# A fused transformer kernel: the first block's 3-tap convolution in PSUM, and the state space tiles turned through DRAM

## The chip, the cores and the metric

The kernel runs on one core of one Trainium2 chip, as one program. The metric is the device time of one execution in microseconds; differences below are against the kernel before, which already holds its 31-tap convolution (second block) in PSUM.

The engines, as the profile names them: PE (TensorE, matmuls; PEld its weight loads), DVE (VectorE), ACT (ScalarE), POOL (GpSimd), SP (SyncE, here the queue that issues most DMAs). ACT and POOL have DMA queues too.

## The reference

512 tokens, 1024 channels, all float32. The first block has two layers. Layer 0 mixes with a gated MLP and attention; layer 1 with a state space model (S5): 64 groups of 16 channels, each with 64 complex states.

```python
def s5_mixer(u, a_re, a_im, log_dt, b_re, b_im, c_re, c_im, d):
    ...                                   # ab = exp(lambda*dt), bb = discretized B
    bu_re = jnp.einsum('gpc,bsgc->bsgp', bb_re, uf)
    bu_im = jnp.einsum('gpc,bsgc->bsgp', bb_im, uf)
    _, _, xr, xi = lax.associative_scan(_complex_affine_combine, (a_r, a_i, bu_re, bu_im), axis=1)
    y = einsum('gcp,bsgp->bsgc', c_re, xr) - einsum('gcp,bsgp->bsgc', c_im, xi) + d * uf
# layer 1:
g_a, g_b = jnp.split(jax.nn.gelu(y) @ od_w_glu[o], 2, axis=-1)
x = x + g_a * jax.nn.sigmoid(g_b)
# both layers then run
def conv_ffn(x, w_up, conv_w, conv_b, w_down):
    h = x @ w_up                          # 1024 -> 2 * 2816
    hc = conv_b + conv_w[0] * hp[:, 0:seq] + ...   # 3 taps over time, per channel
    g, up = jnp.split(hc, 2, axis=-1)
    return (jax.nn.silu(g) * up) @ w_down
x = x + sigmoid(rms_norm(x) @ ple_w_gate[i]) * (p[i] @ ple_w_proj[i])
```

The second block (SwiGLU FFN, a mixer with retention and a 31-tap convolution, SwiGLU FFN, layer norms) is not touched.

## The kernel before, in words

Activations lie channel-major: a tile `x[k]` is 128 channels x 512 tokens, eight of them. Every large matmul is made of three: activations and weights are split into a rounded high part and a low rest (`split`, L290: ACT rounds, DVE or POOL subtracts; weights in `cook`, L328 and L331), and PE adds high x high, high x low, low x high (`mm_fm`, L354 to L356). PSUM has eight banks of 128 x 512 floats; a tile of `bank()` takes one and gives it back after its last use. Weights come on SP's queue through two raw buffers, one piece ahead (`fetch`, L310).

A scheduler orders the instructions of each engine when the program is built: it takes the order of the code as priority, but pulls ahead what it reckons to be ready earlier. On the chip every engine and every DMA queue runs its list in order.

`conv_ffn` (L812) runs three parts of 8, 8 and 6 channel tiles. In a part, each step `c` makes a pair of tiles: 48 matmuls for the gate half (s=0), 48 for the up half (s=1), each into two banks. DVE multiplies a bank by the norm's row `rb` into an SBUF tile `hs` (L839), ACT makes the newest tap with the bias (L841), DVE adds two taps that read `hs` shifted (L845); ACT makes Silu of the gate half (L849), POOL (DVE in the last step of a part) multiplies the two (L851), and `split` hands the product to the down projection. In layer 0 a callback `side()` inserts the preparation of the state space tables between these steps: mostly POOL products (L1147 to L1151), and on PE the transposes and small matmuls of `finish` (L1108, L1115). The 16 finished tables, 128 x 1920 floats each, are kept in DRAM (`tabs`).

The state space layer runs eight units, one per channel tile, software-pipelined over `t`: `load` (six DMAs on SP bring the unit's tables `tG`, `tE`, `tC`, two buffers each), `drive`, `mid`, `scan`, `emit`, and the first GLU column block for the unit's tile. A unit works on blocks of four tokens: 32 channels x 4 tokens on the partitions, 4 channel groups x 128 blocks along the row. `drive` therefore turns the normed tile `h` (L1215) into `up` by 16 copies of 32x128 (L1222, L1224); `mid` multiplies by `tG` on PE (L1231) and rotates on DVE (L1234 to L1237) and POOL (L1239, L1240); `scan` runs two scans on DVE (L1250) and rotates back on DVE and POOL (L1256 to L1261); `emit` sums three matmuls (L1269) and turns the result back inside 16 Gelus of 32x128 (L1274), then splits it into `G`. The first GLU column block (both halves, s=1 and s=0, 12 matmuls per unit) accumulates unit by unit in four banks; blocks 1 to 3 follow densely, then sigmoid, product and addition to `x` (L1319 to L1321), then `conv_ffn` of layer 1.

Of the kernel before, what the change touches and what calls it, by code (L numbers as in the profile page):

```python
# [18 lines left out]
P = 128  # L19
T = 512  # L20
# [29 lines left out]
def tile_net(ctx: ExitStack, tc: tile.TileContext, a, out):  # L50
# [764 lines left out]
    def conv_ffn(l, X, rms, side):  # L815
        Xn = None
        with tc.tile_pool(name=nm("ffn"), bufs=1) as fp:
            rb = None
            for t0, nt in PARTS:
                A = act_tiles(fp, "A", nt)  # L820
                for c in range(nt // 2):
# [12 lines left out]
                    for j in range(2):  # L834
                        cv = []
                        for s in range(2):
                            ch = s * KF + m0 + j
                            hs = fp.tile([P, T], F32, tag=f"hs{s}", name=nm("hs"), bufs=2)
                            vec.tensor_tensor(hs, accs[s][j], rb, op=ALU.mult)  # L839
# [10 lines left out]
                        eng = vec if c == nt // 2 - 1 else pool  # L850
                        eng.tensor_tensor(cv[0], cv[0], cv[1], op=ALU.mult)  # L851
                        split(A.h[2 * c + j], A.l[2 * c + j], cv[0])
# [95 lines left out]
    tabs = [dr.tile([P, 2 * TAB], F32, tag=f"tab{i}", name=f"tab{i}") for i in range(16)]  # L948

# [241 lines left out]
    with tc.tile_pool(name="s5r", bufs=1) as rp:  # L1191
        G = act_tiles(rp, "G", KD)
# [4 lines left out]
        class Unit:  # L1197
# [14 lines left out]
            def drive(self):  # L1212
                k = self.k
                h = rp.tile([P, T], F32, tag="h", name=nm("h"))
                vec.scalar_tensor_tensor(h, x[k], col("norm_mix", KD + k), rb2, op0=ALU.mult, op1=ALU.mult)  # L1215
                hv = h.rearrange("p (n j) -> p j n", j=4)
                self.up = up = rp.tile([P, 4, P], F32, tag="up", name=nm("up"), bufs=3)
                for b in range(4):
                    for i in range(4):
                        d, s = up[32 * b:32 * b + 32, i, :], hv[32 * i:32 * i + 32, 3 - b, :]  # L1220
                        if k < 3 and i % 2:
                            vec.tensor_copy(d, s)  # L1222
                        else:
                            act.copy(d, s)  # L1224

            def mid(self):
                k, up = self.k, self.up
                pv = [bank((P, 4, P)) for _ in range(2)]
                for z in range(2):
                    for i in range(4):  # L1230
                        pe.matmul(pv[z][:, i, :], self.G[:, i, P * z:P * z + P], up[:, i, :], start=True, stop=True)  # L1231
                er, ei = self.E[:, :, 0:P], self.E[:, :, P:]
                t = self.t = [xt_(f"X{'hl'[self.par]}{j}") for j in range(4)]
                vec.tensor_tensor(t[0], er, pv[0], op=ALU.mult)  # L1234
                vec.tensor_tensor(t[1], ei, pv[1], op=ALU.mult)
                vec.tensor_tensor(t[2], er, pv[1], op=ALU.mult)
                vec.tensor_tensor(t[3], ei, pv[0], op=ALU.mult)  # L1237
                eng = pool if k else vec
                eng.tensor_tensor(t[0], t[0], t[1], op=ALU.add)  # L1239
                eng.tensor_tensor(t[2], t[2], t[3], op=ALU.subtract)  # L1240
                self.rm = xt_(f"X{'hl'[self.par]}5")
                vec.tensor_copy(self.rm, r4[:, 4 * k:4 * k + 4].unsqueeze(2).to_broadcast([P, 4, P]))
                pool.memset(self.rm[:, :, 0:1], 0.0)

            def scan(self):
                k, t = self.k, self.t
                er, ei = self.E[:, :, 0:P], self.E[:, :, P:]
                zr, zi = xt_("Xh4"), xt_("Xl4")
                for z, w in ((zr, t[0]), (zi, t[2])):
                    vec.tensor_tensor_scan(z.rearrange("p i n -> p (i n)"), self.rm.rearrange("p i n -> p (i n)"),  # L1250
                                           w.rearrange("p i n -> p (i n)"), 0.0, op0=ALU.mult, op1=ALU.add)
# [4 lines left out]
                vec.tensor_tensor(t[1], er, zr, op=ALU.mult)  # L1256
                vec.tensor_tensor(t[3], ei, zi, op=ALU.mult)
                (pool if k % 3 else vec).tensor_tensor(self.xr[:, :, 1:], t[1], t[3], op=ALU.subtract)
                pool.tensor_tensor(t[0], er, zi, op=ALU.mult)
                pool.tensor_tensor(t[2], ei, zr, op=ALU.mult)  # L1260
                pool.tensor_tensor(self.xi[:, :, 1:], t[0], t[2], op=ALU.add)  # L1261

            def emit(self):
# [6 lines left out]
                y = rp.tile([P, T], F32, tag="y", name=nm("y"), bufs=2)  # L1270
                yv = y.rearrange("p (n j) -> p j n", j=4)
                for i in range(4):
                    for r in range(4):
                        act.activation(yv[32 * i:32 * i + 32, r, :], py[32 * r:32 * r + 32, i, :],  # L1274
                                       AF.Gelu_apprx_tanh)
                split(G.h[k], G.l[k], y)

        units = [Unit(k) for k in range(KD)]
        units[0].load()
        units[0].drive()  # L1280
        acc0, w0s = {}, {}
        for t in range(KD + 3):
            if t + 1 < KD:
# [3 lines left out]
            if t + 1 < KD:  # L1287
                units[t + 1].drive()
            if 0 <= t - 1 < KD:
                units[t - 1].scan()  # L1290
            if t == 2:
                for s in (1, 0):
                    w0s[s] = W(hold=s == 0)
                    acc0[s] = [bank() for _ in range(2)]
            if 0 <= t - 2 < KD:
                units[t - 2].emit()
            if 0 <= t - 3 < KD:
                k = t - 3
                for s in (1, 0):
                    mm_fm(acc0[s], w0s[s], G, [k], start=k == 0, stop=k == KD - 1, js=[k])  # L1300
            if t == KD:
# [4 lines left out]
                fetch(nxt[0] + 1)  # L1306

        X = new_x()
        rms = Rms()
        for c in range(4):  # L1310
# [5 lines left out]
            for j in range(2):  # L1316
# [4 lines left out]
                vec.tensor_tensor(x[m], x[m], sg, op=ALU.add)  # L1321
# [490 lines left out]
```

## Time and profile before

| | us |
|---|---|
| median of 3 runs (lowest, highest) | 2843.62 (2843.29, 2844.3) |
| profiled execution, device time | 2841.44 |
| its span (first to last instruction) | 2839.7 |
| PE busy | 2725.4 (96%) |
| DVE busy | 1628.6 (57%) |
| ACT busy | 1075.9 (38%) |
| POOL busy | 729.5 (26%) |
| mean granted TensorE clock | 0.98 |

The profile is of one execution. Busy is the share of time in which an engine has an instruction in work; PE's matmuls overlap, so PE can be busy without being at its peak. [...] In rows, `a<-b,c` is the written tile and the tiles read, a number after `x` is a count, and square brackets hold the idle time before an instruction and what ended it. Times of day are us from the span's start. The chain of waits follows the work that ended last backwards, at each step to whatever released it.

### The profile page before, as it was taken

How to read it: one execution, taken by the hardware profiler on the slowest of the kernel's cores; microseconds unless marked ns; L12 is line 12 of the kernel's file. 1: busy time of each engine (PE TensorE's matmuls, PEld its weight loads, DVE VectorE, ACT ScalarE, POOL GpSimd, SP SyncE). 2: the span in 40 equal slices, each digit the busy share in tenths (PEclk: the TensorE clock that was granted, in tenths of full speed). 3: DMA queues.
4: the chain of work that ended last, by engine and by line, in shares of the span. 5: the costliest groups of instructions: out<-in, count | busy, mean ns of one | idle time of the engine just before them, and what ended most of it. 6: DMA issues, size and time to landing. Idle time of an engine off the chain costs nothing.

```text
span 2839.7 us, 35255 instructions
## 1 busy us (share of the span) xinstructions
PE 2725.4 (96%) x14363; PEld 2297.3 (81%) x14363; DVE 1628.6 (57%) x2527; ACT 1075.9 (38%) x1503; POOL 729.5 (26%) x621
## 2 busy tenths in 40 slices
PE   9999999999679999999999998999999899999998
PEld 8978887877567888888888887887888778889898
DVE  6456968685774655466333336866387664733335
ACT  5544424344594433244312124333333253431222
POOL 2214046772351001012000025343443321300000
PEclk9999999999689999999999999999999999999999
DMA  5203323433532223224232222222222223232222
GB/s 159 75 30 105 111 95 138 151 124 133 191 97 97 96 89 104 89 89 134 89 104 90 97 82 73 86 95 80 95 80 95 75 89 104 76 104 89 90 90 75
DMA packets 266323, 281.44 MB, mean 99 GB/s; under 512 B 18917, under 2 KB 257479, under 8 KB 266160
## 3 DMA queue, kind: packets, MB, share of 16 engines
q1 hardware_dynamic: 246992, 256.18, 27.4%
q10 hardware_dynamic: 18336, 22.58, 2.2%
q8 instruction: 113, 1.85, 0.3%
q0 software_dynamic: 832, 0.41, 0.1%
q14 instruction: 50, 0.41, 0.0%
HBM read 259.23 MB, written 19.92 MB: 98 GB/s over the span
## 4 chain that ended last, share of the span: by engine, by line
PE 82%; DVE 6%; POOL 5%; ACT 4%; issue 2%; DMA 1%; SPq 0%; POOLq 0%; ACTq 0%; DVEq 0%
PE ps L355 22%; PE ps L354 22%; PE ps L356 22%; PE ps L363 4%; PE ps L365 4%; PE ps L364 4%; ACT y L1274 2%; DVE ps L1478 1%; ACT up L1224 1%; POOL abd L1151 1%; POOL tb L1147 1%; POOL tb L1148 1%; POOL tabs L1151 1%; PE ps L635 1%; PE ps L1539 1%
## 5 line engine op out<-in xcount | busy, mean ns | idle before, releaser
L328 ACT CAST whi<-raw 128x2048 fp32r<-128x2048 f32 (+2 forms) x216 | 406.1, 1880 | 733.5 <-PE ps L355 569.1
L354 PE MATMUL ps<-Xh,whi 128*128 128x512 f32 (+1 forms) x1472 | 570.9, 389 | 3.3 <-ACT whi L328 1.8
L355 PE MATMUL ps<-Xl,whi 128*128 128x512 f32 (+1 forms) x1472 | 566.6, 385 | 3.5 <-POOL Xl L294 3.4
L356 PE MATMUL ps<-Xh,wlo 128*128 128x512 f32 (+1 forms) x1472 | 565.9, 385 | 2.4 <-DVE wlo L331 2.4
L331 DVE TENSOR_TENSOR wlo<-raw,whi 128x2048 fp32r<-128x2048 f32 (+2 forms) x167 | 381.4, 2284 | 321.5 <-ACT whi L328 317.7
L331 POOL TENSOR_TENSOR wlo<-raw,whi 128x2048 fp32r<-128x2048 f32 (+1 forms) x49 | 223.3, 4556 | 688.5 <-ACT whi L328 376.7
L354 PEld LDWEIGHTS ps<-Xh,whi 128*128 128x128 f32 x1472 | 278.5, 190 | 62.2 <-issue 3.1
L355 PEld LDWEIGHTS ps<-Xl,whi 128*128 128x128 f32 x1472 | 279.3, 190 | 60.6 <-POOL Xl L294 4.5
L356 PEld LDWEIGHTS ps<-Xh,wlo 128*128 128x128 f32 x1472 | 279.0, 190 | 60.4 <-DVE wlo L331 3.6
L355 PE MATMUL ps<-XBl,whi 128*128 128x512 f32 (+1 forms) x736 | 282.7, 385 | 3.0 <-POOL XBl L294 3.0
L354 PE MATMUL ps<-XBh,whi 128*128 128x512 f32 (+1 forms) x736 | 281.8, 384 | 1.4 <-ACT XBh L291 1.4
L356 PE MATMUL ps<-XBh,wlo 128*128 128x512 f32 (+1 forms) x736 | 281.5, 383 | 0.0
L355 PE MATMUL ps<-Al,whi 128*128 128x512 f32 (+1 forms) x528 | 203.3, 385 | 3.3 <-DVE Al L294 3.2
L354 PE MATMUL ps<-Ah,whi 128*128 128x512 f32 (+1 forms) x528 | 203.1, 387 | 2.8 <-ACT Ah L291 2.8
L356 PE MATMUL ps<-Ah,wlo 128*128 128x512 f32 (+1 forms) x528 | 202.6, 384 | 0.0
L1478 DVE SCALAR_TENSOR_TENSOR ps<-glu,par,ps 128x512 f32<-128x512 f32 x232 | 174.2, 751 | 4.2
L355 PEld LDWEIGHTS ps<-XBl,whi 128*128 128x128 f32 x736 | 139.2, 189 | 32.4 <-POOL XBl L294 4.0
L354 PEld LDWEIGHTS ps<-XBh,whi 128*128 128x128 f32 x736 | 138.7, 189 | 29.5 <-ACT XBh L291 1.8
L356 PEld LDWEIGHTS ps<-XBh,wlo 128*128 128x128 f32 x736 | 138.9, 189 | 28.1
L363 PE MATMUL ps<-whi,Xh 128*128 128x256 f32 (+1 forms) x512 | 147.8, 289 | 0.5 <-ACT z L597 0.4
L364 PE MATMUL ps<-wlo,Xh 128*128 128x256 f32 (+1 forms) x512 | 144.9, 284 | 0.0
L365 PE MATMUL ps<-whi,Xl 128*128 128x256 f32 (+1 forms) x512 | 144.2, 283 | 0.0
(476 smaller groups left out, 4952.6 us busy)
## 6 DMA issues: line engine op xcount, KB each, us to landing
raw<-in_ffn_w_up_dram SPq DMA_DIRECT2D x66, 1024.0 KB, 5.1
raw<-in_w_in_dram SPq DMA_DIRECT2D x40, 1024.0 KB, 5.1
raw<-in_ffn_w_down_dram SPq DMA_DIRECT2D x32, 1024.0 KB, 4.8
raw<-in_ffn_w_gate_dram SPq DMA_DIRECT2D x22, 1024.0 KB, 5.2
tab<-tabs ACTq DMA_DIRECT2D x16, 960.0 KB, 4.0
raw<-in_ffn_w_down_dram SPq DMA_DIRECT2D x16, 768.0 KB, 4.2
raw<-in_ev_w_in_dram SPq DMA_DIRECT2D x8, 1024.0 KB, 5.3
raw<-in_ple_w_gate_dram SPq DMA_DIRECT2D x8, 1024.0 KB, 4.8
```

The lines of the kernel that those rows point to most:

```text
L328: cp = act.copy(hi, rv)
L331: lo.tensor_tensor(lw, rv, hi.bitcast(F32), op=ALU.subtract)
L354: pe.matmul(acc, wh[j][:, s], X.h[k], start=start and t == 0, stop=False)
L355: pe.matmul(acc, wh[j][:, s], X.l[k], start=False, stop=False)
L356: pe.matmul(acc, wl[j][:, s], X.h[k], start=False, stop=stop and t == len(ks) - 1)
L363: pe.matmul(acc, X.h[k][:, s], wh[j], start=start and t == 0, stop=False)
L364: pe.matmul(acc, X.h[k][:, s], wl[j], start=False, stop=False)
L365: pe.matmul(acc, X.l[k][:, s], wh[j], start=False, stop=stop and t == len(ks) - 1)
L635: pe.matmul(s[:, :nk], qz[2 * self.pp + self.e][:, qs], kT[self.pp][:, :nk], start=True, stop=False)
L1151: pool.tensor_tensor(dst(sl, g), w1[sl, :, :n], w2[sl, :, :n], op=op)
L1274: act.activation(yv[32 * i:32 * i + 32, r, :], py[32 * r:32 * r + 32, i, :], AF.Gelu_apprx_tanh)
L1478: vec.scalar_tensor_tensor(x[m] if t == 30 else acc, u[:, t:t + T], col("ck", t * KD + m), acc, op0=ALU.mult, op1=ALU.add)
```

## The change

It has two parts.

In `conv_ffn` the product with `rb` is written back to its PSUM bank; ACT and the taps read it there. The product of Silu and up half goes to DVE in every step and is written to the gate half's bank, from which `split` reads.

In the state space layer `drive` writes `h` with its tokens regrouped, and ACT's queue stores it to a DRAM tile `hdr[k]`; a new step `lift` reads it back on SP's queue with four DMAs, one per token of a block, which place 32 partitions each. `emit` makes one Gelu of 128x512, stores it to `hdr[k]`, and reads it back with four DMAs; a new step `land` splits what arrived. All eight `drive` stand before the loop, and the `lift` too. `mid` and `scan` keep their sums in the PSUM banks; products of `scan` move to POOL and one subtraction alternates between DVE and POOL. In the loop only the s=1 half of the first GLU block is accumulated; the s=0 half follows after it. The tokens of `G` stay regrouped, so the addition to `x` uses a regrouped view.

```diff
@@ -835,8 +835,8 @@
                         cv = []
                         for s in range(2):
                             ch = s * KF + m0 + j
-                            hs = fp.tile([P, T], F32, tag=f"hs{s}", name=nm("hs"), bufs=2)
-                            vec.tensor_tensor(hs, accs[s][j], rb, op=ALU.mult)
+                            hs = accs[s][j]
+                            vec.tensor_tensor(hs, hs, rb, op=ALU.mult)
                             o = fp.tile([P, T], F32, tag=f"cv{s}", name=nm("cv"), bufs=2)
                             act.activation(o, hs, AF.Identity, scale=col("cw", (l * 3 + 2) * 44 + ch),
                                            bias=col("ffn_conv_b", l * 44 + ch))
@@ -847,9 +847,9 @@
                                                          op0=ALU.mult, op1=ALU.add)
                             cv.append(o)
                         act.activation(cv[0], cv[0], AF.Silu)
-                        eng = vec if c == nt // 2 - 1 else pool
-                        eng.tensor_tensor(cv[0], cv[0], cv[1], op=ALU.mult)
-                        split(A.h[2 * c + j], A.l[2 * c + j], cv[0])
+                        gu = accs[0][j]
+                        vec.tensor_tensor(gu, cv[0], cv[1], op=ALU.mult)
+                        split(A.h[2 * c + j], A.l[2 * c + j], gu)
...
+    hdr = [dr.tile([P, 4, P], F32, tag=f"hd{k}", name=f"hd{k}") for k in range(KD)]
...
-        G = act_tiles(rp, "G", KD)
+        G = Act([None] * KD, [None] * KD)
...
             def drive(self):
-                k = self.k
-                h = rp.tile([P, T], F32, tag="h", name=nm("h"))
-                vec.scalar_tensor_tensor(h, x[k], col("norm_mix", KD + k), rb2, op0=ALU.mult, op1=ALU.mult)
-                hv = h.rearrange("p (n j) -> p j n", j=4)
-                self.up = up = rp.tile([P, 4, P], F32, tag="up", name=nm("up"), bufs=3)
+                h = rp.tile([P, 4, P], F32, tag="h", name=nm("h"), bufs=2)
+                vec.scalar_tensor_tensor(h, x[self.k].rearrange("p (n j) -> p j n", j=4), col("norm_mix", KD + self.k),
+                                         rb2.rearrange("p (n j) -> p j n", j=4), op0=ALU.mult, op1=ALU.mult)
+                nc.scalar.dma_start(hdr[self.k], h)
+
+            def lift(self):
+                self.up = rp.tile([P, 4, P], F32, tag=f"Gh{self.k}", name=nm("up"))
+                src = hdr[self.k].rearrange("(i c) j n -> j c i n", c=32)
                 for b in range(4):
-                    for i in range(4):
-                        d, s = up[32 * b:32 * b + 32, i, :], hv[32 * i:32 * i + 32, 3 - b, :]
-                        if k < 3 and i % 2:
-                            vec.tensor_copy(d, s)
-                        else:
-                            act.copy(d, s)
+                    nc.sync.dma_start(self.up[32 * b:32 * b + 32], src[3 - b])
...
-                pv = [bank((P, 4, P)) for _ in range(2)]
+                self.pv = pv = [bank((P, 4, P)) for _ in range(2)]
...
                 er, ei = self.E[:, :, 0:P], self.E[:, :, P:]
-                t = self.t = [xt_(f"X{'hl'[self.par]}{j}") for j in range(4)]
-                vec.tensor_tensor(t[0], er, pv[0], op=ALU.mult)
-                vec.tensor_tensor(t[1], ei, pv[1], op=ALU.mult)
-                vec.tensor_tensor(t[2], er, pv[1], op=ALU.mult)
-                vec.tensor_tensor(t[3], ei, pv[0], op=ALU.mult)
-                eng = pool if k else vec
-                eng.tensor_tensor(t[0], t[0], t[1], op=ALU.add)
-                eng.tensor_tensor(t[2], t[2], t[3], op=ALU.subtract)
+                t0, t1 = [xt_(f"X{'hl'[self.par]}{j}") for j in range(2)]
+                vec.tensor_tensor(t0, er, pv[0], op=ALU.mult)
+                vec.tensor_tensor(pv[0], ei, pv[0], op=ALU.mult)
+                vec.tensor_tensor(t1, er, pv[1], op=ALU.mult)
+                vec.tensor_tensor(pv[1], ei, pv[1], op=ALU.mult)
+                vec.tensor_tensor(pv[1], t0, pv[1], op=ALU.add)
+                vec.tensor_tensor(pv[0], t1, pv[0], op=ALU.subtract)
                 self.rm = xt_(f"X{'hl'[self.par]}5")
-                vec.tensor_copy(self.rm, r4[:, 4 * k:4 * k + 4].unsqueeze(2).to_broadcast([P, 4, P]))
+                act.copy(self.rm, r4[:, 4 * k:4 * k + 4].unsqueeze(2).to_broadcast([P, 4, P]))
...
             def scan(self):
-                k, t = self.k, self.t
+                k = self.k
                 er, ei = self.E[:, :, 0:P], self.E[:, :, P:]
-                zr, zi = xt_("Xh4"), xt_("Xl4")
-                for z, w in ((zr, t[0]), (zi, t[2])):
+                zr = rp.tile([P, 4, P], F32, tag=f"Gl{k}", name=nm("zr"))
+                zi = rp.tile([P, 4, P], F32, tag="zi", name=nm("zi"), bufs=2)
+                for z, w in ((zr, self.pv[1]), (zi, self.pv[0])):
                     vec.tensor_tensor_scan(z.rearrange("p i n -> p (i n)"), self.rm.rearrange("p i n -> p (i n)"),
                                            w.rearrange("p i n -> p (i n)"), 0.0, op0=ALU.mult, op1=ALU.add)
                 self.xr = rp.tile([P, 4, P + 1], F32, tag="xr", name=nm("xr"), bufs=2)
                 self.xi = rp.tile([P, 4, P + 1], F32, tag="xi", name=nm("xi"), bufs=2)
                 pool.memset(self.xr[:, :, 0:1], 0.0)
                 pool.memset(self.xi[:, :, 0:1], 0.0)
-                vec.tensor_tensor(t[1], er, zr, op=ALU.mult)
-                vec.tensor_tensor(t[3], ei, zi, op=ALU.mult)
-                (pool if k % 3 else vec).tensor_tensor(self.xr[:, :, 1:], t[1], t[3], op=ALU.subtract)
-                pool.tensor_tensor(t[0], er, zi, op=ALU.mult)
-                pool.tensor_tensor(t[2], ei, zr, op=ALU.mult)
-                pool.tensor_tensor(self.xi[:, :, 1:], t[0], t[2], op=ALU.add)
+                t = [xt_(f"X{'hl'[self.par]}{j}") for j in (2, 3)]
+                pool.tensor_tensor(t[0], er, zr, op=ALU.mult)
+                pool.tensor_tensor(t[1], ei, zi, op=ALU.mult)
+                (vec if k % 2 else pool).tensor_tensor(self.xr[:, :, 1:], t[0], t[1], op=ALU.subtract)
+                v = [rp.tile([P, 4, P], F32, tag=f"v{j}", name=nm("v")) for j in range(2)]
+                pool.tensor_tensor(v[0], er, zi, op=ALU.mult)
+                pool.tensor_tensor(v[1], ei, zr, op=ALU.mult)
+                pool.tensor_tensor(self.xi[:, :, 1:], v[0], v[1], op=ALU.add)
...
             def emit(self):
                 k = self.k
...
-                y = rp.tile([P, T], F32, tag="y", name=nm("y"), bufs=2)
-                yv = y.rearrange("p (n j) -> p j n", j=4)
+                g = rp.tile([P, 4, P], F32, tag="h", name=nm("g"), bufs=2)
+                act.activation(g, py, AF.Gelu_apprx_tanh)
+                nc.scalar.dma_start(hdr[k], g)
+                self.y = rp.tile([P, 4, P], F32, tag="y", name=nm("y"), bufs=2)
+                src = hdr[k].rearrange("(r c) i n -> i c r n", c=32)
                 for i in range(4):
-                    for r in range(4):
-                        act.activation(yv[32 * i:32 * i + 32, r, :], py[32 * r:32 * r + 32, i, :],
-                                       AF.Gelu_apprx_tanh)
-                split(G.h[k], G.l[k], y)
+                    nc.sync.dma_start(self.y[32 * i:32 * i + 32], src[i])
+
+            def land(self):
+                k = self.k
+                G.h[k], G.l[k] = [rp.tile([P, T], F32R, tag=f"G{z}{k}", name=nm(f"G{z}")) for z in "hl"]
+                split(G.h[k], G.l[k], self.y.rearrange("p r n -> p (r n)"))
...
-        units[0].drive()
+        for u in units:
+            u.drive()
+        units[0].lift()
+        units[1].load()
+        for u in units[1:]:
+            u.lift()
         acc0, w0s = {}, {}
-        for t in range(KD + 3):
-            if t + 1 < KD:
+        for t in range(KD + 4):
+            if t and t + 1 < KD:
                 units[t + 1].load()
             if t < KD:
                 units[t].mid()
-            if t + 1 < KD:
-                units[t + 1].drive()
             if 0 <= t - 1 < KD:
                 units[t - 1].scan()
             if t == 2:
                 for s in (1, 0):
                     w0s[s] = W(hold=s == 0)
-                    acc0[s] = [bank() for _ in range(2)]
+                acc0[1] = [bank() for _ in range(2)]
+            if 0 <= t - 3 < KD:
+                units[t - 3].land()
             if 0 <= t - 2 < KD:
                 units[t - 2].emit()
-            if 0 <= t - 3 < KD:
-                k = t - 3
-                for s in (1, 0):
-                    mm_fm(acc0[s], w0s[s], G, [k], start=k == 0, stop=k == KD - 1, js=[k])
+            if 0 <= t - 4 < KD:
+                k = t - 4
+                mm_fm(acc0[1], w0s[1], G, [k], start=k == 0, stop=k == KD - 1, js=[k])
             if t == KD:
                 plan[nxt[0]][5] = [(xp, "Xh6"), (xp, "Xl6"), (xp, "Xh7"), (xp, "Xl7"),
                                    (xp, "st_b"), (xp, "st_s"), (xp, "Xh4"), (xp, "Xl4")]
                 plan[nxt[0]][6] = True
                 cook(nxt[0])
                 fetch(nxt[0] + 1)
+        acc0[0] = [bank() for _ in range(2)]
+        mm_fm(acc0[0], w0s[0], G, K8)
...
                 vec.tensor_tensor(sg, sg, acc0[0][j], op=ALU.mult)
-                vec.tensor_tensor(x[m], x[m], sg, op=ALU.add)
+                xv = x[m].rearrange("p (n r) -> p r n", r=4)
+                vec.tensor_tensor(xv, xv, sg.rearrange("p (r n) -> p r n", r=4), op=ALU.add)
```

## Rows read from the trace of the kernel before

**Rows 1.** The page, part 2: PE's busy tenths in 40 slices of 71 us

```profile
PE   9999999999679999999999998999999899999998
```

**Rows 2.** Stretches: length; busy PE, PEld, DVE, ACT, POOL (count); PE clock, DMA share, GB/s

```profile
728.60:861.00 132.40, 85.97 (x419) 71.57 (x420) 94.94 (x121) 106.77 (x251) 63.94 (x61) 0.77 0.42 137
730.00:740.00 10.00, 4.97 (x20) 4.41 (x20) 7.54 (x19) 6.06 (x15) 0.00 (x0) 0.53 1.05 364
790.00:800.00 10.00, 8.53 (x39) 6.54 (x40) 8.33 (x10) 9.67 (x24) 3.36 (x7) 0.83 0.45 147
870.00:880.00 10.00, 10.00 (x45) 8.04 (x44) 0.00 (x0) 1.20 (x2) 0.00 (x0) 1.00 0.34 108
```

**Rows 3.** Chain of waits, 690 to 900: shares by line, then pieces (start, length)

```profile
by line: ACT y L1274 20.8%; ACT up L1224 14.2%; PE ps L354 12.8%; PE ps L355 12.7%; PE ps L356 12.5%; PE ps L1269 3.7%; PE ps L1231 3.2%; issue 2.9%; DMA tE<-tab 2.3%; DVE up L1222 2.1%; ACT wr L291 1.0%; ACT whi L328 0.9%; ACT Gh L291 0.9%
...
728.64 0.76 DVE h L1215
...
732.43 3.79 PE ps L1231 x16
...
755.29 5.05 PE ps L1269 x22
...
837.61 2.69 PE ps L1269 x24
```

**Rows 4.** Groups by line, ACT, 728.6 to 861: count, busy us, mean ns, idle before

```profile
L1274 ACT ACTIVATE y<-ps 32x128 f32<-32x128 f32 x128 | 50.4, 393 | 1.9 <-PE ps L1269 0.3
L1224 ACT COPY up<-h 32x128 f32<-32x128 f32 x104 | 43.5, 418 | 22.1 <-PE ps L1269 13.5 <-DVE h L1215 7.2
```

**Rows 5.** ACT in order of time, the splits of units 1 and 4: start, length

```profile
790.17 0.62 ACT L291 CAST Gh<-y 128x512 fp32r<-128x512 f32 x1
...
832.16 0.62 ACT L291 CAST Gh<-y 128x512 fp32r<-128x512 f32 x1
```

**Rows 6.** Groups by line, DVE, 728.6 to 861

```profile
L1250 DVE TENSOR_TENSOR_SCAN s<-s,s 128x512 f32<-128x512 f32 x16 | 24.4, 1547 | 0.5 <-POOL s L1239 0.4
L1257 DVE TENSOR_TENSOR s<-tE,s 128x512 f32<-128x512 f32 x8 | 13.0, 1626 | 0.0
...
L1234 DVE TENSOR_TENSOR s<-tE,ps 128x512 f32<-128x512 f32 x8 | 5.4, 678 | 0.7 <-PE ps L1231 0.7
```

**Rows 7.** Groups by line, POOL, 728.6 to 861

```profile
L1259 POOL TENSOR_TENSOR s<-tE,s 128x512 f32<-128x512 f32 x8 | 14.8, 1855 | 23.3 <-DVE s L1250 23.3
...
L1239 POOL TENSOR_TENSOR s<-s,s 128x512 f32<-128x512 f32 x7 | 8.9, 1274 | 26.0 <-DVE s L1235 26.0
```

**Rows 8.** PE in order of time: one unit's first matmuls; the GLU block's last

```profile
782.35 2.71 PE L1231 MATMUL ps<-up,tG 128*128 128x128 f32 x16
...
860.81 0.40 PE L356 MATMUL ps<-Gh,wlo 128*128 128x512 f32 x1
```

**Rows 9.** DMA issues, 640 to 870: count, KB each, median us to landing

```profile
tG<-tab SPq DMA_DIRECT2D x16, 256.0 KB, 3.4
...
pjd<-Xl ACTq DMA_DIRECT2D x4, 256.0 KB, 3.8
pjd<-Xh ACTq DMA_DIRECT2D x2, 256.0 KB, 6.4
```

**Rows 10.** SP's queue in order of time

```profile
726.97 1.27 SPq L1209 DMA_DIRECT2D tG<-tab  x2
```

**Rows 11.** Whom PE waited for, 250 to 730: total us, times, longest

```profile
PE ps L1115 <- POOL tabs L1151: 9.8, 5, 3.1
```

**Rows 12.** One stretch of the first FFN

```profile
456.00:478.00 22.00, 18.99 (x98) 15.46 (x99) 17.20 (x29) 8.51 (x12) 18.21 (x24) 0.84 0.44 163
```

**Rows 13.** Groups by line, 240 to 700

```profile
L845 DVE SCALAR_TENSOR_TENSOR cv<-hs,par,cv 128x511 f32<-128x511 f32 (+1 forms) x88 | 69.7, 817 | 0.6
...
L851 POOL TENSOR_TENSOR cv<-cv,cv 128x512 f32<-128x512 f32 x16 | 22.2, 1399 | 69.8 <-DVE cv L845 40.8 <-ACT cv L849 23.3 <-ACT whi L328 3.3
```

**Rows 14.** The page's groups: the accumulating taps of the 31-tap convolution

```profile
L1478 DVE SCALAR_TENSOR_TENSOR ps<-glu,par,ps 128x512 f32<-128x512 f32 x232 | 174.2, 751 | 4.2
```

## The prediction

> **What bounds the kernel now.** I read the page first. The 40 slices show TensorE at 9 nearly everywhere; the two weak ones, the 11th and 12th (6 and 7), are where the state space layer runs [rows 1]. In the second FFN and the whole second block PE is at 9 in almost every slice; to win there, work has to leave PE, and this change takes no matmul out.
>
> Second, the busy table of the weak stretch. From 728.6 us (the norm's broadcast row is ready) to 861.0 (last matmul of the first GLU column block) PE is busy 85.97 of 132.4 us at a mean granted clock of 0.77, while ACT is busy 106.77. [...]
>
> Third, the chain of waits over 690 to 900: the two largest shares are ACT's `y` (20.8%) and `up` (14.2%) [rows 3]. They are 128 Gelus and 104 copies of 32x128 that turn the tiles, 50.4 + 43.5 us [rows 4]. Per unit: 16 x 0.393 + 16 x 0.418 + a 0.62 split = 13.6 us. ACT's splits of units stand at 790.17 and, three units later, 832.16: a pace of 14.0 [rows 5]. So in the middle of the stage ACT runs almost without a gap and sets the pace; the others wait for it.
>
> **State space stage.** All sums go against the profiled execution: span 2839.7, device time 2841.44, 2.2 under the median of the runs (2843.62).
>
> *ACT.* Out: 32 small operations per unit. In: one 128x512 copy (`rm`, from DVE), one 128x512 Gelu, two DMA issues. With 0.62 for each 128x512 operation [rows 5] and 0.64 for an issue, as on SP [rows 10]: 3 x 0.62 + 2 x 0.64 = 3.1 us per unit, far off the path. So what is late next?
>
> *DVE per unit.* Before, four products from PSUM at 0.68 [rows 6]. Now six such operations, 4.1; two scans at 1.55, 3.1; half a subtraction (`xr`) and one split, 0.68 to 1.63 each, 1.0 to 2.4. The stage's weight splits, one of 128x2048 and four of 128x512, count as eight of L1234 and add 0.7 per unit: 8.9 to 10.3.
>
> L1257 takes 1.63 on average, L1234 of the same shape 0.68 [rows 6]: the first reads two SBUF tiles while POOL works, the second one SBUF and one PSUM tile. [...] I keep 1.55.
>
> *POOL per unit.* Four products, one addition, half a subtraction: 5.5 operations at 1.27 to 1.86 (as L1259 is delayed now) [rows 7]: 7.0 to 10.2. Before it had five to six, so this hardly grows; but now it counts.
>
> *PE per unit.* 16 + 24 instructions of 128 columns and only the s=1 half of the GLU, 6 matmuls: 2.71 [rows 8] + 2.69 [rows 3] + 6 x 0.227 = 6.8 us at 2.4 GHz. At 1.2 GHz: 3.79 + 5.05 x 24/22 [rows 3] + 2.7 = 12.0.
>
> *DMA and SP per unit.* Two tables (1.97 MB by their shape) as before, plus for the Gelu's turn a write and four reads, together 0.52 MB, and some 0.5 MB of weights. At the 364 GB/s of 730 to 740 [rows 2] 3.0 MB take 8.2 us; if the reads in runs of 512 B go at half that rate, 9. (The `h` turns come once, at the start.) SP issues 10 DMAs at 0.64 [rows 10], 6.4.
>
> *Coupling.* Tables are double buffered: POOL's four products release `tE` (5.1), the load is issued and lands (1.3 + 3.4 [rows 9]), DVE makes its products and a scan (4.1 + 1.5): 15.4 us for two units.
>
> Five bounds between 7 and 10 and none at 14. I take **9.5 us** a unit, near DVE's, range 8 to 12 (12: PE at 1.2 GHz).
>
> *Start.* Before, PE starts at 732.43, 3.8 after `h` [rows 3]. Now `h` goes through DRAM: 0.76 + issue 0.64 + write 3.8 (6.4 in the other row) + four reads issued 2.6, landed 3.4 [rows 3, 9, 10] = 11.2: PE at 740, DVE at 742. The eight `h` have two buffers and come first in the program: four pairs of 0.76 + 0.64 + 3.8 = 21 us would hold DVE until 749, since all of its queue stands behind a waiting `h`. I take 745, and after six products and a scan POOL's first product at 750 (746 to 754). `h` now reads `x` with a step of four elements, which no row prices at this shape: nothing to twice 0.76, inside these waits.
>
> *Tail.* POOL ends at 750 + 8 x 9.5 = 826. Then PE has the last emit (2.7), the s=1 rows of three units (18 x 0.227 = 4.1) and all 48 matmuls of s=0 (10.9): 17.7 us, end at 843.7. The last Gelu's way round (2.7 + 0.62 + 0.64 + 3.8 + 2.6 + 3.4 + 1.3 = 15.1) is covered by the 14.9 us of PE work that needs no result of it; without that cover it costs up to 12. Against 861.0: **17 us gained** (pace 8: 29; pace 12: 3 lost; the start 4 either way).
>
> **Convolution from PSUM.** A tap on SBUF takes 0.817 us in the first FFN [rows 13], an accumulating tap that reads and writes PSUM 0.751 [rows 14]: the switch costs nothing by itself, and the taps lose POOL as a neighbour.
>
> [...]
>
> The product `gu` moves from POOL (16 x 1.40 in layer 0 [rows 13]) to DVE: 16 x 0.68 = 11 us there, less 88 x 0.07 = 6 on the taps. In layer 0 PE waits 9.8 us in five places for table pieces from POOL [rows 11], and around 456 to 478 it is busy 18.99 of 22 us at a clock of 0.84, some 3 us more [rows 12]. POOL's queue is in order: a `gu` that waits for Silu holds the table work behind it. Between nothing and all of this (0 to 12) I credit **4 us**. The other sign: a pair's four banks, of eight, are now held until the split rather than the first product, and the tables want two. DVE's work for a pair is 4 x 0.68 + 8 x 0.75 + 4 x 0.68 = 11.4 us, beside 96 x 0.227 = 22 of PE; but DVE is busy 17.20 of 22 there [rows 12]: 5 lost at worst. In layer 1 PE has no gap, and both effects are nothing.
>
> **Sum.** 2841.4 - 17 - 4 = 2820.4, plus 2.2 to the median: **2822.6 us**.
>
> **Rivals.**
> (B) DMA takes ACT's place: 11 to 12 us a unit. For it: 8 to 9 us of bytes, and the turns' short runs, which no row prices. Against: over the stage now 137 GB/s [rows 2]. POOL's end 838 to 846, stage end 856 to 864, with the FFN's 4 a gain of 1 to 9: about 2838.
> (C) PE stays at 1.2 GHz, as at 730 to 740: 740 + 8 x 12.0 = 836, then s=0 and the rest partly at half clock, about 16: 852. Against: in 790 to 800 the clock is 0.83 with PE busy 8.53 of 10 [rows 2], and the load rises to 6.8 of 9.5. Gain 9 + 4: about 2831.
> (D) PE stalls for PSUM banks in layer 0. It decides once DVE needs more than the 22 us of a pair; at 2.5 us in each of 11 pairs 27 us, more than the stage gives: 2854. Against: DVE's 5 us of room.
> (E) SP's queue puts the reads that wait for a Gelu's write ahead of a table load for the unit two later. Then a loop closes: emit 2.7, Gelu, issue and write 5.1, reads 2.6, load 4.7, DVE 5.6, POOL 7: 27.7 us for two units, 13.9 each. POOL's end 861, stage end 879, 18 lost: about 2857. For it: both are on one queue in order. Against: in the order of the code the reads stand ahead of the load for four units later only, 7 us a unit.
>
> **How the numbers follow.** Forecast 0.62 (own range 2806 to 2838), B 0.15, C 0.09, D 0.08, E 0.06. The time is the forecast's, rounded: 2822. Eight in ten: 2802 (pace 8, an early start, 8 from the FFN) to 2848 (B, C and the milder part of D). Under 0.2% (5.7 us) can't be told from no change. Faster by more: 0.62, and 0.09 of B, 0.08 of C, 0.01 of D = 0.80. Slower: 0.06 of D, 0.06 of E = 0.12. Same: 0.08.
>
> **What would show it.** ACT's busy time in the stage falls from 107 to about 30; DVE and POOL are the chain there; units are 9 to 10 apart; POOL's first product stands near 750; PE has work after the last emit; the waits for table pieces in layer 0 shrink. It is wrong if units stay 12 or more apart, if DVE stands before `h` past 749, if PE waits for DVE or ACT in the FFNs (banks), or if SP waits for a write with table loads behind it.

## The result and the profile after

The changed kernel takes **2821.2 us** (median, 2815.4 to 2822.4) against 2844.0 for the kernel before in the same rounds: ratio 0.9915, 95% interval [0.9898, 0.9932]. The forecast was 2822 (2802 to 2848). The total came out right, but two of its terms were wrong in opposite directions: the experiments below measure each half alone.

The profiled execution is the quickest of the four, 2815.4 us, with a span of 2813.6. First its first FFN: whom TensorE waited for between 250 and 730 us (total, times, longest), then the stretch of [rows 12] and the state space stage from the norm's row to the end of the first GLU block, with the part between GpSimd's first and last product and the part before it, and last TensorE where that block ends (from 836.18 on it reads `wr`, the next block's weights):

```profile
PE ps L1230 <- DMA up<-hd: 12.9, 1, 12.9
PE ps L1116 <- POOL tabs L1152: 2.3, 1, 2.3
```

```profile
456.00:478.00 22.00, 22.00 (x97) 18.00 (x96) 20.05 (x33) 9.46 (x13) 7.55 (x11) 1.00 0.41 140
715.40:836.30 120.90, 72.64 (x417) 63.68 (x418) 75.05 (x90) 22.09 (x32) 60.35 (x62) 0.76 0.72 220
741.20:819.30 78.10, 48.22 (x302) 42.82 (x302) 56.38 (x68) 16.24 (x24) 60.30 (x62) 0.77 0.75 224
715.40:741.20 25.80, 7.50 (x32) 6.97 (x32) 13.71 (x16) 0.00 (x0) 0.02 (x1) 0.57 0.85 279
```

```profile
835.95 0.39 PE L356 MATMUL ps<-Gh,wlo 128*128 128x512 f32 x1
836.18 0.40 PE L354 MATMUL ps<-Gh,wr 128*128 128x512 f32 x1
```

The waits for table pieces, 9.8 us in five places [rows 11], are one of 2.3, and TensorE is unbroken at a granted clock of 1.00, as a share of full speed, where it had 18.99 of 22 us at 0.84. The stage begins at 715.4 instead of 728.6, 13.2 us earlier, and these come from the FFN. The stage itself takes 120.9 instead of 132.4 us [rows 2]: 11.5. (The other 1.4 us between the two profiled executions lie behind it.) ACT's busy time there falls from 106.77 to 22.09. None of the engines is full in what is left; the DMA share rose from 0.42 to 0.72.

The page's row of TensorE tenths (part 2; compare [rows 1]) still has its two weak slices at the state space stage:

```profile
PE   8999999999579999999999998999999899999998
```

The chain of waits over 715.4 to 835, shares by line, then its five longest pieces (start, length):

```profile
by line: DMA hd<-h 11.7%; DMA tG<-tab 8.2%; DMA tE<-tab 7.6%; POOL v L1260 5.6%; issue 5.5%; POOL s L1256 5.2%; DVE zi L1249 4.9%; POOL v L1261 4.8%; POOL s L1257 4.2%; PE ps L354 3.7%; PE ps L355 3.7%; PE ps L356 3.7%; POOL xi L1262 3.5%; 
...
714.39 4.16 DMA tG<-tab
718.63 6.06 DMA hd<-h
730.32 4.85 DMA hd<-h
781.40 5.81 DMA tE<-tab
798.55 5.61 DMA tG<-tab
```

Where ACT's `y` and `up` stood [rows 3], DMA landings now stand, 27.5% in the three lines at the top; GpSimd's products and the scan `zi` together have as much. In the middle GpSimd idles between units, and what ends its wait is a scan that came late (start, length, line; idle before, releaser):

```profile
780.86 1.26 POOL L1257 TENSOR_TENSOR s<-tE,zi 128x512 f32<-128x512 f32 x1 [5.76 <-DVE zi L1249]
...
787.43 1.28 POOL L1262 TENSOR_TENSOR xi<-v,v 128x512 f32<-128x512 f32 x1
```

The opening on SP's queue, and on VectorE (four of the eight `h` are left out):

```profile
722.62 2.38 SPq L1223 DMA_DIRECT2D up<-hd  x3
725.09 1.48 SPq L1210 DMA_DIRECT2D tE<-tab  x2
726.99 2.60 SPq L1210 DMA_DIRECT2D tC<-tab  x2
729.63 19.08 SPq L1223 DMA_DIRECT2D up<-hd  x28
748.81 1.18 SPq L1210 DMA_DIRECT2D tG<-tab  x2
```

```profile
715.40 2.15 DVE L1215 SCALAR_TENSOR_TENSOR h<-x,par,st_r 128x512 f32<-128x512 f32 x2 [1.90 <-ACT st_r L197]
721.42 1.12 DVE L1215 SCALAR_TENSOR_TENSOR h<-x,par,st_r 128x512 f32<-128x512 f32 x1 [3.87 <-DMA hd<-h]
...
735.26 1.12 DVE L1215 SCALAR_TENSOR_TENSOR h<-x,par,st_r 128x512 f32<-128x512 f32 x1 [0.94 <-DMA hd<-h]
736.30 0.69 DVE L1233 TENSOR_TENSOR s<-tE,ps 128x512 f32<-128x512 f32 x1
```

VectorE stands before `h` for the writes, six times, 12.1 us, and has the last `h` at 736.4, 21.0 us after the stage began (TensorE's sums for the first unit are there at 731.4, and VectorE's first product with them, L1233, starts at 736.30, behind that `h`: its list runs in order); the third unit's `tG` is issued only after 28 lifts of 19.08 us. That is what TensorE and SP wait for longest in the stage:

```profile
PE ps L1230 <- DMA up<-hd: 18.8, 2, 12.9
PE ps L1230 <- DMA tG<-tab: 11.8, 2, 11.0
PE ps L354 <- ACT Gh L291: 11.0, 3, 6.6
PE ps L1270 <- DMA tC<-tab: 3.6, 1, 3.6
...
SPq L1277 <- DMA hd<-g: 20.5, 6, 6.1
SPq L1210 <- PE ps L1270: 11.3, 3, 6.4
```

### The profile page after: what moved, and what is told of

It is laid out like the page before. It is cut to its first block, busy times and chain, and to the rows that moved or that the text cites. A ratio compares the mean times of both kernels' runs of the same rounds, so it can differ in the third digit from the quotient of the medians.

```text
span 2813.6 us, 35122 instructions
## 1 busy us (share of the span) xinstructions
PE 2709.8 (96%) x14363; PEld 2293.3 (82%) x14363; DVE 1608.2 (57%) x2526; ACT 987.6 (35%) x1287; POOL 671.5 (24%) x590
## 4 chain that ended last, share of the span: by engine, by line
PE 86%; DVE 6%; POOL 2%; issue 2%; DMA 2%; ACT 2%; SPq 0%; POOLq 0%; DVEq 0%; ACTq 0%
PE ps L354 23%; PE ps L355 23%; PE ps L356 23%; PE ps L363 4%; PE ps L365 4%; PE ps L364 4%; DVE ps L1491 1%; PE ps L635 1%; PE ps L1552 1%; PE ps L659 1%; DVE x L287 1%; POOL st_b L263 1%; PE ps L1116 1%; DMA hd<-h 0%; ACT whi L328 0%
## 5 line engine op out<-in xcount | busy, mean ns | idle before, releaser
L220 POOL TENSOR_TENSOR st_a<-st_a,st_q 128x512 f32<-128x512 f32 x25 | 44.3, 1770 | 487.9 <-ACT st_q L218 487.8
```

The costliest lines, as they stand in the source:

```text
L220: eng.tensor_tensor(self.acc, self.acc, sq, op=ALU.add)
```

## The experiments

Each was timed beside the kernel before (2844 to 2846 us in every group). Differences between two changed kernels are taken from medians; each ratio's interval is some 3 to 5 us to either side.

**The two halves alone.** e1 is before with the diff's two `conv_ffn` edits; e2 is the changed kernel without them.

> The kernel before with the two edits of conv_ffn alone (the scaled sum hs stays in its PSUM bank, and the product gu is made by VectorE in that bank); the S5 stage is as before. Theory, that the two halves of the change add up: the S5 stage starts 13 us earlier and is as long as before (132 us), so 2831 us, ratio 0.9954. Rival, that the 13 us are lost when the S5 stage is the old one (its ScalarE-bound units take back what comes early): 2840 to 2844 us.

> The changed kernel with the two conv_ffn edits undone, so that only the S5 stage is new. Theory, that the halves add up: the stage starts at about 728.6 us as before and lasts about 119 us instead of 132, so 2844 less 13 is 2831 us. Rival, that the new stage's gain depends on the early state of the queues that the FFN edits leave: 2836 to 2844 us.

e1: 2829.9 us, ratio 0.9946 [0.9934, 0.9959], 14.2 us gained. e2: 2834.4, 0.9963 [0.9950, 0.9977], 9.6 gained. They add up to 23.8 against 22.8 for both, so the halves add up within the intervals. e1 comes out as its theory said; e2's median lies between its theory's 2831 and its rival's 2836. By medians the stage is worth 9 to 10 us; the 11.5 of the trace belongs to a quick execution.

**The FFN's two edits apart.** e3 keeps only `hs` in PSUM, e4 only the move of `gu`:

```
 e3:  hs = accs[s][j];  vec.tensor_tensor(hs, hs, rb, op=ALU.mult)
 e4:  vec.tensor_tensor(cv[0], cv[0], cv[1], op=ALU.mult)      # was eng = pool
```

> The kernel before with one edit: hs is scaled in its PSUM bank and the taps read it there; the product gu stays on GpSimd. Theory, that the 13 us of the FFN layer come from GpSimd's queue, where 21 of 22 products stood ahead of the table work that TensorE waits for: TensorE's waits for tabs stay at 8 us or more of the 9.8, the gain is 0 to 4 us (2840 to 2844). Rival, that they come from VectorE's sources leaving SBUF, so that GpSimd beside it runs faster: the table waits fall under 5 us and the gain is 9 to 13 us (2831 to 2835).

> The kernel before with one edit: the product gu moves from GpSimd to VectorE, still in SBUF; hs and the taps stay in SBUF. Theory of GpSimd's queue: the table waits of TensorE fall from 9.8 us to under 5 and the gain is 9 to 13 us (2831 to 2835). Rival of SBUF sources: VectorE now has more SBUF work, the table waits stay and the gain is 0 to 4 us, or the kernel is slower.

e3: 2832.8, 0.9960 [0.9948, 0.9973], 11.3 gained. e4: 2835.5, 0.9968 [0.9956, 0.9981], 8.6 gained. Each theory had one of them do nearly nothing. TensorE's waits and VectorE's taps, first e3, then e4:

```profile
PE ps L1115 <- POOL tabs L1151: 2.9, 2, 2.4
...
L845 DVE SCALAR_TENSOR_TENSOR cv<-ps,par,cv 128x511 f32<-128x511 f32 x44 | 32.1, 744 | 0.7
```

```profile
PE ps L1114 <- POOL tabs L1150: 4.3, 4, 2.2
...
L845 DVE SCALAR_TENSOR_TENSOR cv<-hs,par,cv 128x511 f32<-128x511 f32 x44 | 35.3, 813 | 0.3
```

Either edit ends more than half of the waits. In e4 GpSimd has no `gu`. In e3 it still has all 16 (16 of 22, not the 21 of e3's expectation) and idles as long ahead of them as before (69.7 us at L851, 69.8 in [rows 13]; the part put down to the taps falls from 40.8 to 25.4). But the taps are shorter, and the `tb` products of L1148 take 566 and 524 ns instead of 757 and 585. So neither the place of `gu` nor the sources of the taps is the whole cause: each alone gains. By the medians they overlap, 11.3 + 8.6 against 14.2 for both together, though the intervals allow a plain sum. How much of e3's gain comes from VectorE's shorter taps and how much from GpSimd's shorter products is not separated.

**PSUM sources in the stage.** e12 writes the sums of `mid` to SBUF, so that the scans read SBUF:

```
+vec.tensor_tensor(t0, t0, pv[1], op=ALU.add)        # was pv[1], t0, pv[1]
+vec.tensor_tensor(t1, t1, pv[0], op=ALU.subtract)   # was pv[0], t1, pv[0]
```

> The changed kernel with the sums of mid written to two SBUF tiles instead of back into the PSUM banks, so that the scans read SBUF as before the change; everything else of the change stays. Rival that the stage's gain comes from PSUM sources: the scans go from 1.20 back to about 1.5 us while GpSimd works, each unit's chain is 0.6 us longer and GpSimd's products slower, so 5 to 10 us are lost on the changed kernel (2826 to 2831). Theory, that the gain came from taking the turning copies off ScalarE and that the pace now is set by DMA latency and the queues: the scans are slower as said, but 0 to 3 us are lost (2821 to 2824).

2825.2, 0.9932 [0.9919, 0.9946]: 4.0 us above the changed kernel's median (4.8 by the ratios), between the two expectations; every run (2824.2 to 2827.0) is above its slowest, though the intervals overlap. The scans and the longest-waiting GpSimd product, the changed kernel, then e12:

```profile
L1249 DVE TENSOR_TENSOR_SCAN zi<-s,ps 128x512 f32<-128x512 f32 x8 | 9.7, 1206 | 0.0
L1249 DVE TENSOR_TENSOR_SCAN zr<-s,ps 128x512 f32<-128x512 f32 x8 | 9.6, 1199 | 0.0
...
L1257 POOL TENSOR_TENSOR s<-tE,zi 128x512 f32<-128x512 f32 x8 | 10.2, 1273 | 36.3 <-DVE zi L1249 36.3
```

```profile
L1250 DVE TENSOR_TENSOR_SCAN zr<-s,s 128x512 f32<-128x512 f32 x8 | 13.8, 1725 | 0.0
L1250 DVE TENSOR_TENSOR_SCAN zi<-s,s 128x512 f32<-128x512 f32 x8 | 10.8, 1347 | 0.0
...
L1258 POOL TENSOR_TENSOR s<-tE,zi 128x512 f32<-128x512 f32 x8 | 13.5, 1692 | 38.3 <-DMA up<-hd 27.8 <-DVE zi L1250 10.5
```

A scan costs 1.54 us on average from SBUF and 1.20 from PSUM, and GpSimd's product beside it 1.69 with the one and 1.27 with the other. Single scans from SBUF take anything from 1.19 to 2.31 us in the kernel before (16 scans, median 1.22), from PSUM all take 1.19 to 1.22 in the changed one: the average of 1.55 [rows 6] is made by the long ones. By the medians nearly half of the stage's gain of 9 to 10 us hangs on this. That the rest comes from taking the turns off ACT is what the chain of waits says; no run has the turns through HBM without the stage's other edits.

**What sets the stage's opening.** e5 gives each `h` a buffer; e6 lifts two units ahead, inside the loop:

```
 e5:  h = rp.tile(..., tag="h", bufs=2) if self.k < 2 else xt_(one of six free tags)
 e6:  -for u in units[1:]: u.lift()     +units[1].lift()
      in the loop, after mid:           +if t + 2 < KD: units[t + 2].lift()
```

> The changed kernel with a buffer of its own for each of the eight h (six of them lie in tiles that stand free then), so that VectorE doesn't wait for the writes to HBM. Theory, that the opening is set by those writes only in part, since the 28 lifts ahead of the third unit's tables on SP's queue remain: VectorE's 12.1 us of waiting for hd go, mid(0) starts 2 to 6 us earlier, and the kernel gains 0 to 4 us. Rival, that VectorE's wait is what delays the whole opening: 6 to 12 us.

> The changed kernel with the lifts of units 2 to 7 moved into the loop, two units ahead of their use, so that the third unit's tables no longer stand behind 28 lifts on SP's queue. Theory, that this queue sets the opening: TensorE's 11.0 us wait for tG before mid(2) shrinks under 4 us and the kernel gains 4 to 9 us. Rival, that in the loop the lifts stand behind SP's waits for hd<-g and for tC's buffer, and the later units start late: no gain or a loss of up to 5 us.

e5: 2817.8, 0.9906 [0.9893, 0.9920], 3 us by the medians; the interval overlaps the changed kernel's, so this can't be told from nothing. VectorE's wait for `hd` is gone from its list, but TensorE's first wait for `up<-hd` grew from 12.9 to 16.1, and VectorE waits 9.2 for what it makes: most of the wait moved. GpSimd's first product comes 22.9 us after the stage began, instead of 25.8. e6: 2838.0, 0.9977 [0.9968, 0.9986], 17 us lost, far more than its rival allowed. TensorE's wait for `tG` before `mid(2)` did shrink there, from 11.0 to 1.5, so the lifts ahead of the table were its cause; the loss is further on. The chain of waits shows a loop (start, length):

```profile
784.53 3.03 PE ps L1270 x24
...
787.57 0.52 SPq L1210
...
788.14 0.61 SPq L1210
...
788.79 5.71 DMA tG<-tab
...
794.64 3.75 PE ps L1230 x16
798.39 2.92 PE ps L1270 x24
...
801.33 0.52 SPq L1210
```

SP issues `tC` when TensorE's emit frees its buffer, and `tG` behind it; it lands, `mid` and the next emit follow: 787.57 to 801.33, 13.8 us for this unit. GpSimd's mean pace is 11.9. In the changed kernel SP's queue has two `tG` ahead of the first `tC` that waits; that the loop therefore doesn't close there is read from the order of the queue, no run tests it.

**What sets the pace.** e7 has three buffers for `tG` and `tE` (and, to make room, `zi` and `v` in free tiles); e8 issues the reads of `y` from ScalarE's queue; e10 moves the loads of `tC`; e11 is e8 and e10; e9 is all of these with e5's buffers, loads two units ahead, and the third unit's tables ahead of 24 lifts.

```
 e7:  tag="tG", bufs=3    tag="tE", bufs=3
 e8:  -nc.sync.dma_start(self.y[...], src[i])   +nc.scalar.dma_start(self.y[...], src[i])
 e10: after emit in the loop:  +if 2 <= t < KD: units[t].load_c()
```

> The changed kernel with three buffers instead of two for tG and tE (zi and v lie in tiles that stand free then, to make room). If the loads' wait for a free buffer sets the pace: GpSimd's 9.76 us a unit falls to 8 to 8.8, a gain of 5 to 12 us. Rival, that SP's queue itself, held by its waits for hd<-g (20.5 us) and for tC's buffer (11.3 us), sets when the loads are issued: the pace stays within 0.4 us of 9.76 and the gain is under 3 us.

> The changed kernel with the reads of y issued on ScalarE's queue instead of SP's, so that SP no longer waits for hd<-g ahead of the next tables. If SP's queue sets the pace: it falls from 9.76 to 8.5 to 9.2 us a unit, a gain of 4 to 9 us. Rival, that the buffers or the engines set it: a gain under 2 us, or a loss where ScalarE's own work (rm, the splits of G, Gelu) now stands behind the wait for hd<-g.

> The changed kernel with one thing moved: the tables tC(t) of units 2 to 7 are loaded at the end of loop step t instead of with tG and tE at the start of step t-1. There the load stood on SP's queue waiting for TensorE's emit of two units before, and the reads of y and the next tG stood behind it. Theory, that this wait sets the pace (in the run with the lifts in the loop the chain of waits went round emit, tC's issue, tG, mid, emit at 14.4 us a unit): SP's 11.3 us of waits on TensorE's emit shrink under 4 us and the kernel gains 3 to 8 us on the changed one (2813 to 2818). Rival, that SP's wait for hd<-g, which ScalarE's queue relieved by 7 us, is the only one that counts: 0 to 2 us.

> The late loads of tC and the reads of y on ScalarE's queue together. If the two waits on SP's queue are both in the path, the gains add: 7 + 3 to 8 us, so 2806 to 2811 us. Rival, that one hides the other (whichever goes, the same next limit shows: GpSimd's and VectorE's work at about 8.5 us a unit or the DMA engines): 2811 to 2815 us.

> The changed kernel with all of it: three buffers for tG and tE with the loads issued two units ahead, the third unit's tables issued before 24 of the lifts, tC loaded late, y read on ScalarE's queue, and eight buffers for h. Theory, that the table's latency and SP's order set the pace and the opening, not the engines: TensorE's 11.0 us wait before mid(2) goes, the pace falls to 8 to 8.8 us a unit and the kernel takes 2797 to 2808 us. Rival, that the DMA engines are near their limit (0.73 of the stage before, 26.5 MB in 119 us), so what is issued earlier lands later: 2808 to 2815 us.

| kernel | us | ratio to before | 95% | GpSimd's pace, us a unit |
|---|---|---|---|---|
| changed | 2821.2 | 0.9915 | [0.9898, 0.9932] | 9.8 |
| e7 | 2818.9 | 0.9911 | [0.9897, 0.9924] | 10.0 |
| e8 | 2813.8 | 0.9897 | [0.9882, 0.9912] | 9.7 |
| e10 | 2818.6 | 0.9906 | [0.9891, 0.9920] | 9.5 |
| e11 | 2815.0 | 0.9892 | [0.9878, 0.9907] | 8.8 |
| e9 | 2814.0 | 0.9893 | [0.9876, 0.9909] | 9.3 |

The pace is that of the one profiled execution: from GpSimd's first product to the end of its last `xi`, by eight. It is the quickest execution of the kernel in the changed kernel, e8, e10 and e11, the slowest in e7. The two pieces in the changed kernel, e8 and e11:

```profile
741.18 1.26 POOL L1257 TENSOR_TENSOR s<-tE,zi 128x512 f32<-128x512 f32 x1 [27.27 <-DVE zi L1249]
817.74 1.59 POOL L1262 TENSOR_TENSOR xi<-v,v 128x512 f32<-128x512 f32 x1
...
740.35 1.26 POOL L1257 TENSOR_TENSOR s<-tE,zi 128x512 f32<-128x512 f32 x1 [27.37 <-DVE zi L1249]
816.58 1.59 POOL L1262 TENSOR_TENSOR xi<-v,v 128x512 f32<-128x512 f32 x1
...
741.68 1.26 POOL L1264 TENSOR_TENSOR s<-tE,zi 128x512 f32<-128x512 f32 x1 [27.50 <-DVE zi L1256]
810.60 1.59 POOL L1269 TENSOR_TENSOR xi<-v,v 128x512 f32<-128x512 f32 x1
```

e7: a third buffer alone can't be told from none; its rival holds. e8: 7 us by the medians (5 by the ratios), with intervals that overlap. But the 8.5 to 9.2 us a unit that its theory wanted didn't come: the pace is 9.7 as before, and what the trace shows as shorter is the part behind GpSimd's last `xi`, 15.1 us instead of 17.0. e10 ends SP's wait for the emit (11.3 us to 1.1), but the wait for `hd<-g` behind it grows from 20.5 to 33.2: again the wait moved, and the gain can't be told from nothing. e11 and e9 add nothing to e8 in the total, which is what their rivals said. In e11's trace, though, with both of SP's waits relieved, the pace is 8.8, the lowest of all, and the stage takes 115.1 us against 118.8 in e8. That points to the two waits holding the pace together; but e9, which relieves both too, has 9.3, and e11's median shows nothing of it, so these single traces don't settle it. In e9 TensorE's 11.0 us before `mid(2)` is gone, yet GpSimd's first product stands at 741.6 (741.2 in the changed kernel). Its opening:

```profile
715.40:740.00 24.60, 5.83 (x32) 5.67 (x32) 14.75 (x20) 0.00 (x0) 0.00 (x0) 0.65 0.95 320
```

The DMA engines are busy 0.95 of it at 320 GB/s: more issued early lands no earlier. That these bytes are the floor of the opening fits, but no run took bytes away to show it. e8, e9 and e11 are the quickest versions, clearly faster than before; against the changed kernel their medians are 6 to 7 us lower, with intervals that overlap.

## Why the prediction was right, and where it wasn't

**The sum.** Forecast: 17 from the stage and 4 from the FFN. Measured by the halves alone: 9.6 and 14.2. The time is right because the errors, 7 too much and 10 too little, nearly cancel: the total is right by luck.

**The FFN's term was mis-sized**, 4 for 13 to 14. The mechanism named (table work held in GpSimd's queue, TensorE slowed by the gaps) is what the trace shows; I took a third of the bound's 12. The waits went from 9.8 to 2.3, 7.5 us, and 456 to 478 at 1.00 instead of 0.84 is at most 22 x 0.16 = 3.5 us more; some 2 of the 13.2 are not assigned. What I left out is e3's part: "the taps lose POOL as a neighbour" stood in the text, counted as time of VectorE alone, and the edit that does it is worth 11.3 us by itself. In layer 1 nothing came, as forecast: from the last matmul of the four GLU blocks to the end it is 1912.6 us before and 1912.6 in e1. Rival D (banks) didn't come: no wait of TensorE for VectorE's banks is among those of 250 to 717.

**The stage's start** was forecast 21.4 us after `h`; GpSimd's first product came 25.8 after (741.2). The two buffers of `h` did hold VectorE, and longer than forecast. The sum in the prediction gave 21 us for the four pairs, and the last `h` is indeed there 21.0 us after the stage began; but I took 745, which is 16.4 after 728.6, without a reason. These 4.6 us cover the error of the start, 4.4. e5 shows what the hold is worth: without it the first product is only 2.9 us earlier, since TensorE then waits longer for its lift. The table on SP's queue behind 28 lifts, which I didn't count as late, cost TensorE another 11.0 before the third unit.

**The pace** was forecast 9.5 and is 78.1 / 8 = 9.76, but for another reason. I put it near VectorE's 8.9 to 10.3. VectorE is busy 56.38 of 78.1 us, 7.0 a unit, and GpSimd 7.5: neither sets it. The sign of being wrong that the prediction named last came: SP waits for `hd<-g`, 20.5 us, with table loads behind it. That is a part of rival E's mechanism, without its price of 13.9 a unit: relieving this wait alone (e8) leaves the pace at 9.7, relieving the wait for the emit alone (e10) at 9.5, both together at 8.8 (e11) and 9.3 (e9). These are single traces; what sets the pace is left open. A closed loop of 13.8 stands in e6, but it goes through the buffer of `tC` and not, like rival E's, through the reads of `y`. Rival B's 11 to 12 didn't come; its cause, transfers in ACT's place, did in part: `tG` lands in 4.9 us instead of 3.4 [rows 9] (medians). The half rate supposed for reads in runs of 512 B was my assumption, and no run shows it: between GpSimd's first and last product the DMA engines moved 224 GB/s at a share of 0.75.

**The tail** was forecast 17.7 and is 836.3 - 819.3 = 17.0, with TensorE busy 16.91 of it. Start, pace and tail are off by 4.4 + 2.1 - 0.7 = 5.8: that is 17.3 against 11.5 in the profiled execution. The other 2 us are between it and the medians' 9.6.

**Clock.** The traces give the clock as a share of full speed; no run shows the 1.2 and 2.4 GHz by which the prediction's sums name the shares 0.5 and 1.00. The 0.227 us of a matmul in those sums is 44 weight loads, one to each matmul of 512 columns, in 10 us at 1.00 [rows 2]; the 12.0 us a unit at half clock was my estimate. Rival C's clock came in the opening: 0.57 from 715.4 to 741.2, where TensorE is busy 7.50 of 25.8 us. It did not stay: 0.77 between GpSimd's first and last product and 1.00 in the tail. Nor did TensorE become the limit of the pace, being busy 48.22 of those 78.1 us.

**Operands in PSUM.** Scans from PSUM take 1.20 against 1.55 [rows 6] and 1.54 in e12, 0.34 less each. The sum kept 1.55, so it had some 0.7 a unit too much for VectorE; e12 measures 4 us for the stage. The taps from PSUM take 743 ns on average against 817 [rows 13], and 744 in e3 with that one edit. The difference is again made by long ones: the median tap is 745 ns from SBUF, with single ones up to 1047, and 743 from PSUM, where none is above 752. So the PSUM source cost the taps nothing, as the sum had it.

## What to carry to other kernels

Where VectorE and GpSimd work side by side, price an edit that takes a VectorE operand out of SBUF on both engines: here that edit alone was worth 11 us in one FFN, where TensorE's waits named only GpSimd. When a turn by an engine becomes a turn through HBM, write down the issue order of the one queue that carries it and mark each entry that must wait: here TensorE waited 11.0 us for a table load behind 28 reads, and taking one such wait away lengthened the next (12.9 to 16.1 us in e5, 20.5 to 33.2 in e10). Compare times counted from the stage's own start: here a start 13 us earlier makes a hold that lasted longer than forecast look shorter. Time each half of a two-part change alone before believing that a right total had right terms.

## What the runs showed of the hardware that was not expected

- `h` computed from `x` and `rb`, both read with a step of four elements: 1.12 us on VectorE for 128x512, against 0.76 in order [rows 3].
- In the stage, where GpSimd works beside VectorE, single scans with two SBUF sources take 1.19 to 2.31 us (the kernel before; mean 1.55, and 1.54 in e12), and with one source in PSUM 1.19 to 1.22 (the changed kernel): the mean is made by the long ones.
- 28 issues of 64 KB on SP took 19.08 us, 0.68 each, waits between them included.
